# Output projection: the turned rows of the later token tiles go through two 512-column halves in the big accumulators

## The chip, the cores and the metric

The kernel runs on one core of a Trainium2 chip. The metric is the time of one execution on the device, in microseconds (us), as the median of several runs. The engines of a core are named as in the profile: PE is TensorE's matmul stream and PEld its weight loads, DVE is VectorE, ACT is ScalarE, POOL is GpSimd, and SP issues transfers. SBUF is the on-chip memory that the engines work from, PSUM the accumulators that PE writes, and DRAM the device's main memory.

## What is computed

One layer of a streaming encoder, for a prompt of 2048 tokens and for 8 x 16 sample tokens (one tile of 128), of 1024 columns each. Two token mixers (a chunked band attention and an mLSTM) give 512 columns each; the change lies in the product of the joined 1024 columns with `w_out` and the normalisation after it:

```python
h = rms_norm(x, norm_g[0])
z = h @ w_in
...
att = rms_norm(att, g_att)                      # 512 columns
...
mlstm_out = (hb * g_mlstm * sigmoid(ob))        # 512 columns
mix = jnp.concatenate([att, mlstm_out], axis=-1) @ w_out
x = x + rms_norm(mix, norm_g[1])
ffn, new_buf = conv_ffn(rms_norm(x, norm_g[2]), conv_buf, w_up, w_conv, b_conv, w_down)
x = x + rms_norm(ffn, norm_g[3])
```

All data is in 32-bit floats.

## The kernel before

The program runs through three stages, in about this order of time: the input projection with the attention and the mLSTM beside it (to about 1040 us), the output projection (`project`, about 1040 to 1306 us), and the feed-forward in three blocks of tokens.

A product of 32-bit numbers is made of three matmuls (`mm3`, lines 111 to 113): each operand is split into a high part, which ScalarE writes as a copy in a shorter format, and a low part, which VectorE writes as the difference. The three matmuls are high by high, high by low and low by high.

`project` goes through 17 tiles of 128 tokens, in the order 0 to 7, the sample tile (number 16, `SAMPLE`), 8 to 15. For one tile it does this:

- `load` brings the tile's 1024 columns into SBUF (`m`, in the trace `mr`). At tile 8 it first finishes the attention and mLSTM work and opens the pools of the feed-forward (`open_ffn`).
- `norm` takes the square sum of the 512 attention columns on ScalarE (L1021), the mean and its root on POOL (L94, L100), and scales those columns on VectorE (L1023).
- `turn_rows` turns the tile, since a matmul needs the contracted columns on the partitions: 8 transposes of 128 x 128 on PE (L83) into an accumulator, then the high part by a copy on ScalarE (L218) and the low part by a subtraction on VectorE (L219), both into `mt`.
- For each of two halves of the output columns, 8 x 3 matmuls sum into one 512-column accumulator (`wo` in the trace). Then VectorE multiplies it with the gain into `mx` (L1057), and ScalarE takes its square sum (L1059). The square's by-product is written to a place that is free at the time, `mx` for the first half and `mt` for the second.
- Root (L100), scaling and the residual (L1069), and the store (L1070).

The turn of the next tile is written down between the two halves of the current one. In the same loop `folds` (L1210 to L1217) prepares sums of `w_down` for the feed-forward: POOL issues loads and stores, VectorE adds (L1213). Until tile 8 the last attention and mLSTM work (`ms`, L716 to L733) runs beside the projection.

The accumulators come from one PSUM pool with two places for each kind: `ps_mm` gives 512 columns (tag `mm`) and `ps_big` 1024 (tag `big`). The projection's own accumulators are always `ps_mm`. `rows_to_T` takes the kind as `bank`: with `ps_big` itself it turns all 8 blocks into one accumulator and copies and subtracts 1024 columns at a time; with any other function it goes in two groups of four blocks, each with an accumulator, a copy and a subtraction of 512. Before the change tiles 0 to 7 use `ps_mm`, and the sample tile (number 16) and 8 to 15 use `ps_big`. The feed-forward uses `ps_big` for its accumulators `uec`, the attention for its scores and their transposes.

The order of the instructions on each engine is not that of the source: a planner lays it out when the program is built, from the source's order as priority and its own estimates of times, except where `keep_in_program_order` holds it. Each engine then works through its list in order. A tile in a place of a pool waits until the last reader of the place's former tile is done.

Of the kernel before, what the change touches and what calls it, by code (L numbers as in the profile page):

```python
# [50 lines left out]
def hymba_step(ctx: ExitStack, tc: tile.TileContext, I: dict, O: dict):  # L51
# [12 lines left out]
    def ps_big(name):  # L64
        return psum.tile([P, 1024], F32, tag="big", name=name)
# [16 lines left out]
    def transpose(out, in_, n=P):  # L82
        nc.tensor.transpose(out, in_, ident[:n, :n])  # L83
# [125 lines left out]
    def rows_to_T(hrow, chunk, j, name, bank):  # L209
        w = 4 if bank is not ps_big else KT  # L210
        for q in range(KT // w):
            pt = bank(f"{name}_pt{q}")
            for k in range(w):
                transpose(pt[:, k * P:(k + 1) * P], hrow[:, (w * q + k) * P:(w * q + k + 1) * P])
            ptv = pt.rearrange("p (k t) -> p k t", k=w)
            hv = chunk[:, 0, w * q:w * q + w, j * P:(j + 1) * P]
            lv = chunk[:, 1, w * q:w * q + w, j * P:(j + 1) * P]
            nc.scalar.copy(hv, ptv)  # L218
            nc.vector.tensor_tensor(lv, ptv, hv, op=ALU.subtract)  # L219
# [733 lines left out]

    wo = []
    g1 = []
    gatt = const.tile([P, 4], F32, name="gatt")

    def w_out_steps():
# [39 lines left out]
    def project(tiles):  # L998
# [25 lines left out]
            s.mt = mt[:, :2 * D].rearrange("p (a k n) -> p a k n", a=2, k=KT)  # L1024

        def turn_rows(s):
            rows_to_T(s.m, s.mt, 0, f"mT{s.t}", ps_mm if s.t < 8 else ps_big)

        fold, owed = folds(), [0.0]
        load(ss[0])  # L1030
        norm(ss[0])
        yield 0.0, 0.3
        turn_rows(ss[0])
        load(ss[1])
        yield 0.9, 1.2
        for n_, s in enumerate(ss):
# [7 lines left out]
            for hf in range(2):  # L1044
                c = slice(hf * 512, hf * 512 + 512)
                acc = ps_mm(f"wo{t}_{hf}")
                for k in range(KT):
                    mm3(acc, s.mt[:, 0, k, :], s.mt[:, 1, k, :], wo[k][0][:, c], wo[k][1][:, c],
                        start=(k == 0), stop=(k == KT - 1))
                    if k % 4 == 3:  # L1050
                        owed[0] += FOLD_RATE
                        while owed[0] >= 1:
                            owed[0] -= 1
                            next(fold, None)
                        yield 2.6, 0.5
                ssq = small.tile([P, 1], F32, tag="wssq", name=f"wssq{t}_{hf}")
                nc.vector.tensor_tensor(m[:, c], acc, g1[0][:, c], op=ALU.mult)  # L1057
                idle = m[:, 512:D] if hf == 0 else s.mt[:, 0, 0:4, :].rearrange("p k n -> p (k n)")
                nc.scalar.activation(idle, acc, AF.Square, accum_out=ssq)  # L1059
                if hf == 0:  # L1060
                    ssa = ssq
                    mean_square(ssa, ssq, D)
                    if nxt:
                        turn_rows(nxt)
                        if n_ + 2 < len(ss):
                            load(ss[n_ + 2])
                        yield 0.9, 1.2
# [957 lines left out]
```

## Time and profile before

| | us |
|---|---|
| median of 3 runs | 2727.55 |
| lowest and highest | 2724.9, 2730.89 |
| the profiled execution | 2730.95 |
| its span, first to last instruction | 2729.2 |

| engine | busy us | share of the span |
|---|---|---|
| PE | 2651.2 | 97% |
| DVE | 1862.9 | 68% |
| ACT | 1421.0 | 52% |
| POOL | 692.4 | 25% |

The times are those of one execution on the chip. A busy PE is a modelled figure, since matmuls overlap. In a row of the timeline the brackets hold how long the engine had been idle before the instruction and which instruction (engine, tile, line) released it. In a table by stretches, the columns are the length, the busy time of each engine, the granted clock of TensorE as a share of full speed, the share of the transfer engines, and GB/s. The granted clock over the whole span is 0.993.

### The profile page before, as it was taken

Reading aid. Unit: us, or ns where it says so; the run is one execution under the profiler, and the core shown is the slowest. Engines: PE = TensorE matmul, PEld = TensorE weight load, DVE = VectorE, ACT = ScalarE, POOL = GpSimd, SP = SyncE. Lnnn points to the kernel's source line nnn. Section 1 sums busy time; section 2 is a strip of 40 time slices with the busy share of each in tenths; the row PEclk is TensorE's granted clock in tenths of the full one; section 3 lists DMA queues with packets and bytes.
Section 4 is the critical chain, followed back from the end, with each engine's and each line's share of the span. In section 5 each row is a group of like instructions: output and inputs, shape, how many; then the busy total and the mean of one; then the engine's idle time right before and its main releaser. Section 6 shows DMA issues by size and latency. Waiting matters only on the chain. (4 is left out here: it accounts for less than half of the span.)

```text
span 2729.2 us, 47644 instructions
## 1 busy us (share of the span) xinstructions
PE 2651.2 (97%) x16459; PEld 2474.6 (91%) x16459; DVE 1862.9 (68%) x3519; ACT 1421.0 (52%) x2904; POOL 692.4 (25%) x1325
## 2 busy tenths in 40 slices
PE   7999999999999999999999999999999999999998
PEld 7899989998999998777999997899999878999976
DVE  5444555433556666566899997758888876999956
ACT  4345554433556665333555456655455665555554
POOL 1000001201000001354454551023333212556401
PEclk9999999999999999999999999999999999999999
DMA  5545465457644555598787668767886877798875
GB/s 174 156 124 149 125 183 158 151 155 252 194 139 134 152 151 158 178 294 287 281 241 236 204 206 294 237 187 202 228 220 175 256 237 239 213 253 232 259 250 180
DMA packets 333855, 555.73 MB, mean 204 GB/s; under 512 B 61906, under 2 KB 169518, under 8 KB 333294
## 3 DMA queue, kind: packets, MB, share of 16 engines
q1 hardware_dynamic: 250942, 405.06, 48.2%
q0 software_dynamic: 44080, 113.81, 14.5%
q10 hardware_dynamic: 38592, 33.83, 3.7%
q8 instruction: 129, 2.11, 0.3%
q14 instruction: 112, 0.92, 0.1%
HBM read 390.03 MB, written 172.22 MB: 206 GB/s over the span
## 5 line engine op out<-in xcount | busy, mean ns | idle before, releaser
L111 PE MATMUL uec<-B,wuh 128*128 128x384 f32 (+1 forms) x720 | 235.9, 328 | 5.3 <-DVE ug L1524 3.5
L112 PE MATMUL uec<-B,wuh 128*128 128x384 f32 (+1 forms) x720 | 235.1, 327 | 0.0
L113 PE MATMUL uec<-B,wul 128*128 128x384 f32 (+1 forms) x720 | 234.4, 327 | 0.0
L1353 ACT CAST wuh<-wu 128x512 fp32r<-128x512 f32 x255 | 141.7, 618 | 115.9 <-PE uec L112 113.5
L113 PE MATMUL dn<-wdh,al 128*128 128x512 f32 x462 | 186.8, 404 | 3.2 <-DVE al L1354 3.1
L111 PE MATMUL dn<-wdh,ah 128*128 128x512 f32 x462 | 184.3, 399 | 4.7 <-ACT ah L1353 3.3
L1354 DVE TENSOR_TENSOR al<-ar,ah 128x768 fp32r<-128x768 f32 (+2 forms) x141 | 108.5, 779 | 117.2 <-ACT ah L1353 113.9
L112 PE MATMUL dn<-wdl,ah 128*128 128x512 f32 x462 | 183.1, 396 | 0.0
L1353 ACT CAST ah<-ar 128x768 fp32r<-128x768 f32 (+2 forms) x141 | 96.2, 692 | 151.3 <-PE dnm L112 114.4
L1354 DVE TENSOR_TENSOR wul<-wu,wuh 128x512 fp32r<-128x512 f32 x255 | 164.4, 684 | 2.6 <-ACT wuh L1353 2.4
L111 PE MATMUL vo<-wi_h,hT 128*128 128x256 f32 x544 | 156.5, 288 | 1.9 <-ACT vo_st L244 1.8
L113 PE MATMUL vo<-wi_h,hT 128*128 128x256 f32 x544 | 155.2, 285 | 0.0
L112 PE MATMUL vo<-wi_l,hT 128*128 128x256 f32 x544 | 155.0, 285 | 0.0
L1354 DVE TENSOR_TENSOR wdl<-wdr,wdh 128x512 fp32r<-128x512 f32 x231 | 145.4, 685 | 7.6 <-ACT wdh L1353 7.4
L423 ACT ACTIVATE tmp<-tmp,mn 128x640 f32<-128x640 f32 (+4 forms) x128 | 97.7, 763 | 89.1 <-DVE mn L422 78.0
L111 PEld LDWEIGHTS uec<-B,wuh 128*128 128x128 f32 x720 | 135.1, 188 | 8.1 <-issue 3.5
L422 DVE CUSTOM_DVE_ANT_0 tmp<-s,nb 128x640 f32<-128x640 f32 (+4 forms) x128 | 94.1, 737 | 64.3 <-PE s L412 63.9
L112 PEld LDWEIGHTS uec<-B,wuh 128*128 128x128 f32 x720 | 135.2, 188 | 0.2
L113 PEld LDWEIGHTS uec<-B,wul 128*128 128x128 f32 x720 | 135.1, 188 | 0.0
L1353 ACT CAST wdh<-wdr 128x512 fp32r<-128x512 f32 x231 | 127.4, 620 | 13.2 <-PE uec L112 7.6
L435 DVE TENSOR_TENSOR ptl<-pt,pth 128x640 fp32r<-128x640 f32 (+4 forms) x128 | 93.8, 738 | 58.4 <-ACT pth L434 57.5
L111 PE MATMUL qk<-hT,wi_h 128*128 128x384 f32 (+1 forms) x384 | 128.2, 334 | 0.6 <-ACT gates L293 0.5
(473 smaller groups left out, 8968.6 us busy)
## 6 DMA issues: line engine op xcount, KB each, us to landing
wu<-in_w_up SPq DMA_DIRECT2D x220, 256.0 KB, 5.1
wu<-wsd SPq DMA_DIRECT2D x176, 256.0 KB, 4.9
wdr<-wtd SPq DMA_DIRECT2D x132, 256.0 KB, 5.8
wi_raw<-in_w_in SPq DMA_DIRECT2D x52, 512.0 KB, 4.2
wdr<-in_w_down SPq DMA_DIRECT2D x99, 256.0 KB, 4.6
wsd<-ws POOLq DMA_DIRECT2D x88, 256.0 KB, 4.9
ar<-ad_S SPq DMA_DIRECT2D x50, 384.0 KB, 3.9
kraw<-kTd SPq DMA_DIRECT2D x112, 128.0 KB, 3.3
```

The source lines that it names most:

```text
L111: nc.tensor.matmul(out, ah, bh, start=start, stop=False, skip_group_check=onto)
L112: nc.tensor.matmul(out, ah, bl, start=False, stop=False, skip_group_check=onto)
L113: nc.tensor.matmul(out, al, bh, start=False, stop=stop, skip_group_check=onto)
L422: nc.vector.tensor_tensor_reduce(o_, s_, b_, 1.0, 3e38, ALU.add, ALU.min, accum_out=mn)
L423: nc.scalar.activation(tmp[:, :n], tmp[:, :n], AF.Exp, bias=mn, scale=-1.0, accum_out=rsum[:, i % 4, hh:hh + 1])
L435: nc.vector.tensor_tensor(s.ptl[:, sl, qc], ptv, s.pth[:, sl, qc], op=ALU.subtract)
L1353: nc.scalar.copy(h, r)
L1354: nc.vector.tensor_tensor(l, r, h, op=ALU.subtract)
```

## The change

A constant `TURN_BIG = 4` takes the place of the 8 in `turn_rows`, and `ps_big` itself is no longer passed but a function that returns the first 512 columns of a big accumulator. As `rows_to_T` compares `bank` with `ps_big`, it now takes its other branch for every tile.

```diff
@@ -953,6 +953,7 @@
     wo = []
     g1 = []
+    TURN_BIG = 4
     gatt = const.tile([P, 4], F32, name="gatt")
...
@@ -1024,7 +1025,7 @@
         def turn_rows(s):
-            rows_to_T(s.m, s.mt, 0, f"mT{s.t}", ps_mm if s.t < 8 else ps_big)
+            rows_to_T(s.m, s.mt, 0, f"mT{s.t}", ps_mm if s.t < TURN_BIG else lambda name: ps_big(name)[:, 0:512])
```

So tiles 0 to 3 are as before. Tiles 4 to 7 still go in two groups of four blocks, but each group takes one of the two big accumulators and leaves the second half of it unused. The sample tile and tiles 8 to 15 go in two groups as well, each in a big accumulator of its own, with two copies and two subtractions of 512 columns in place of one each of 1024.

## The prediction

> **What bounds the kernel now.** I read the page's head first, then the busy time by stretches of the output projection, then the timeline of TensorE in that stretch for the idle time that ends at each turn, then ScalarE and VectorE around each of those gaps, and last the stretches behind the projection, to see whether time won there is kept.
>
> ```profile
> span 2729.2 us, 47644 instructions
> PE 2651.2 (97%) x16459; PEld 2474.6 (91%) x16459; DVE 1862.9 (68%) x3519; ACT 1421.0 (52%) x2904; POOL 692.4 (25%) x1325
> ...
> 1110.00:1310.00 200.00, 188.62 (x889) 151.21 (x889) 120.42 (x200) 72.95 (x176) 95.82 (x179) 0.97 0.83 273
> ...
> 1310.00:1330.00 20.00, 17.88 (x92) 17.30 (x92) 18.82 (x25) 11.20 (x15) 6.91 (x9) 0.91 0.81 312
> 1330.00:1550.00 220.00, 217.97 (x1244) 215.92 (x1243) 209.54 (x328) 111.59 (x177) 116.59 (x183) 1.00 0.74 228
> ```
>
> The columns of a stretch are its length, then busy us (and instructions) of PE, PEld, DVE, ACT and POOL, the granted clock, the DMA share and GB/s. TensorE is busy 97% of the span, so only its idle time and its slow time can be won. The change touches tiles 4 to 7, the sample tile and 8 to 15, which are turned between 1110 and 1310 us. There PE is idle 200.00 - 188.62 = 11.4 us, and the granted clock is 0.97. VectorE is at 60% and ScalarE at 36% there. Behind it, from 1330 on, PE is at 99% and VectorE at 95%.
>
> The wait of each turn, by the timeline (start, length, engine, line, and in brackets the idle time before it and what ended it):
>
> ```profile
> 1115.08 0.50 PE L111 MATMUL wo<-wo,mt 128*128 128x512 f32 x1 [0.27 <-DVE mt L219]
> ...
> 1128.54 0.49 PE L716 MATMUL ms<-mqk 128*128 128x128 f32 x2 [0.57 <-DVE num L733]
> ...
> 1144.81 0.66 PE L83 MATMUL mT_pt<-ident,mr 128*128 128x128 f32 x4 [0.65 <-ACT mx L1059]
> ...
> 1159.01 0.66 PE L83 MATMUL mT_pt<-ident,mr 128*128 128x128 f32 x4 [0.71 <-ACT mx L1059]
> 1160.47 0.50 PE L111 MATMUL wo<-wo,mt 128*128 128x512 f32 x1 [0.28 <-DVE mt L219]
> ...
> 1181.22 0.50 PE L111 MATMUL wo<-wo,mt 128*128 128x512 f32 x1 [1.16 <-ACT mt L218]
> 1185.14 0.79 PE L113 MATMUL wo<-wo,mt 128*128 128x512 f32 x1 [2.61 <-DVE mt L219]
> 1199.43 0.50 PE L111 MATMUL wo<-wo,mt 128*128 128x512 f32 x1 [0.46 <-ACT mt L218]
> 1254.04 0.50 PE L111 MATMUL wo<-wo,mt 128*128 128x512 f32 x1 [1.60 <-ACT mt L218]
> 1295.51 0.50 PE L113 MATMUL wo<-wo,mt 128*128 128x512 f32 x1 [0.90 <-DVE mt L219]
> ```
>
> Two kinds are to be seen. In tiles 4 to 7 the second four transposes wait for ScalarE's square of the projection (mx L1059), and the next accumulator waits for the subtraction (mt L219). Both are waits for a place among the two 512-column accumulators, which the turn shares with the projection. From the sample tile on, the matmuls of the next tile wait for the copy (L218) and the subtraction (L219) of its own turned rows.
>
> Where such idle time is long, the clock falls behind it:
>
> ```profile
> 1183.60:1190.40 6.80, 5.26 (x12) 4.13 (x13) 4.84 (x11) 0.00 (x0) 5.69 (x10) 0.51 0.98 387
> 1190.40:1196.40 6.00, 6.00 (x27) 4.82 (x26) 2.76 (x5) 0.69 (x2) 2.16 (x4) 0.99 0.91 269
> ...
> 1255.30:1258.70 3.40, 3.40 (x8) 2.72 (x9) 1.39 (x2) 1.00 (x2) 2.96 (x5) 0.51 1.03 414
> ...
> 1056.65 0.51 PE L111 MATMUL wo<-wo,mt 128*128 128x512 f32 x1 [1.15 <-ACT wo L983]
> ```
>
> Behind the sample tile's gaps the clock is 0.51 for 6.8 us: 12 matmuls take 5.26 us, where the next stretch does 27 in 6.00, so 12 would take 2.67. That is 2.6 us lost. Behind tile 12's gap of 1.60 us, 8 matmuls take 3.40, which at 27 in 6.00 would take 1.78: 1.6 us lost. A single gap of 1.15 (tile 0, at 1056.65) or 0.90 us (tile 15) has no such stretch behind it.
>
> On this the Trainium skill differs ("TensorE: Matmul & The Clock Gate", Part 1): it has the clock halved after at least one idle window of about 3.4 us, and warns of gaps above that. No gap of this stage is that long, so by that rule alone no clock time hangs on these turns and the sum below would be smaller by the two clock terms, -4.1 instead of -8.3; the trace shows the fall behind a gap of 1.60 us, and the trace decides.
>
> **The change part by part.** *Tiles 4 to 7.* The number of instructions stays; only the bank moves, from the 512-column accumulators to the two big ones. Nothing else uses the big ones here:
>
> ```profile
> L435 DVE TENSOR_TENSOR ptl<-pt,pth x128: 274/820/827, 101.6 to 1072.2; 128x640 fp32r<-128x640 f32 x96, 128x128 fp32r<-128x128 f32 x8, 128x256 fp32r<-128x256 f32 x8, 128x384 fp32r<-128x384 f32 x8
> ...
> L111 PE MATMUL uec<-B,wuh x720: 304/336/442, 1306.7 to 2579.8; 128*128 128x384 f32 x120, 128*128 128x320 f32 x60
> ```
>
> The attention read them last at 1072.2 us, and the feed-forward first writes them at 1306.7 (the third and fourth numbers are the first and last start). So the waits for a place go: 0.27 in tile 4, 0.65 in tile 6, 0.71 + 0.28 in tile 7. What is late next is the mLSTM's work on the same engine: in tile 5, where the transposes did not wait, PE stood 0.57 us for num (L733). In tile 7 the same num follows the transposes, so of its 0.99 I count 0.42. Together -1.3; the ends are 0 (num takes all the places) and -2.0 (all four rows).
>
> *The sample tile and 8 to 15.* Eight transposes into 1024 columns, one copy and one subtraction become two times four transposes, copies and subtractions of 512.
>
> ```profile
> L218 ACT CAST mt<-mT_pt x17: 578/1004/1017, 1113.7 to 1291.7; 128x1024 fp32r<-128x1024 f32 x9, 128x512 fp32r<-128x512 f32 x8
> L219 DVE TENSOR_TENSOR mt<-mT_pt,mt x17: 684/1214/1225, 1114.3 to 1294.2; 128x1024 fp32r<-128x1024 f32 x9, 128x512 fp32r<-128x512 f32 x8
> ```
>
> The columns are shortest, median and longest, in ns; the median is here one of the nine long ones, the shortest one of the eight short ones. Two copies of 512 take 2 x 0.58 = 1.16 us against 1.00, two subtractions 2 x 0.68 = 1.37 against 1.21: +0.16 a tile on each engine, +1.4 for nine, on engines that are idle 64% and 40% of the stage. I take 0 for them on the path; if that cover is gone they cost up to 1.4 each. In return the first half is ready sooner: the copy after 0.58 in place of 1.00, and it need wait for four transposes only, and the subtraction of half a row after 0.68 in place of 1.21. The first half feeds k = 0 to 3, 12 matmuls or 12 x 0.222 (27 in 6.00) = 2.7 us, which covers the second half's copy and subtraction.
>
> ```profile
> 1179.03 1.04 PE L83 MATMUL mT_pt<-ident,mr 128*128 128x128 f32 x8
> 1179.38 0.37 ACT L732 ACTIVATE num<-ms,colsp 128x129 f32<-128x129 f32 x1 [3.79 <-DVE cst L731]
> 1180.16 1.01 ACT L218 CAST mt<-mT_pt 128x1024 fp32r<-128x1024 f32 x1 [0.41 <-PE mT_pt L83]
> 1180.51 0.28 DVE L733 TENSOR_TENSOR num<-num,ms 128x129 f32<-128x129 f32 x1
> 1183.19 0.69 DVE L1213 TENSOR_TENSOR fold<-fold,fold 128x512 f32<-128x512 f32 x1 [2.40 <-issue]
> 1183.87 1.22 DVE L219 TENSOR_TENSOR mt<-mT_pt,mt 128x1024 fp32r<-128x1024 f32 x1
> ...
> 1252.99 1.00 ACT L218 CAST mt<-mT_pt 128x1024 fp32r<-128x1024 f32 x1
> 1254.03 1.23 DVE L219 TENSOR_TENSOR mt<-mT_pt,mt 128x1024 fp32r<-128x1024 f32 x1 [1.66 <-ACT mt L218]
> ...
> 1294.24 1.22 DVE L219 TENSOR_TENSOR mt<-mT_pt,mt 128x1024 fp32r<-128x1024 f32 x1
> ```
>
> Sample tile: ScalarE is free at 1179.75, so the first copy ends at 1180.33 in place of 1181.17. The subtraction stood behind a fold (L1213) that came to VectorE 2.40 us after the work before it. With the half ready at 1180.33, it can be queued behind num (ends 1180.79), before that fold, and end at 1181.5; the second half then comes behind the fold, at 1184.56, and holds PE some 0.3 us. The L113 of 1185.14 moves to about 1181.55, less 0.3: -3.3, and with so little idle time left the 2.6 of the slow clock goes too: -5.9. If the fold keeps its place, only 1.22 - 0.69 = -0.5 is left. I take -5.9: at 1252.99 and 1254.03 the subtraction follows its copy at once, as it would here.
>
> Tile 8: the 0.46 goes (-0.46), since the copy gains 0.41 and starts four transposes earlier. Tile 12: the gap of 1.60 shrinks by 1.00 - 0.58 to 1.18, the like of the 1.15 at 1056.65, so the slow clock goes: -0.4 - 1.6 = -2.0; the ends are -0.4 and -3.2 (the gap and its clock). Tile 15: the subtraction is late behind other VectorE work, and its half is 0.53 shorter: -0.5, to -0.9 if it is queued sooner.
>
> Against it stands the switch between transposes and matmuls:
>
> ```profile
> 1198.03 0.48 PE L111 MATMUL wo<-wo,mt 128*128 128x512 f32 x1
> 1198.35 0.39 PE L112 MATMUL wo<-wo,mt 128*128 128x512 f32 x1
> ```
>
> The first matmul behind a turn takes 0.32 to the next where 0.22 is usual: 0.1 more, for nine turns that become two groups each, +0.9. Last, the program's order is made by a planner from its own estimates, and moving these instructions lays the fold, the loads and the weights of the feed-forward anew. I count one new wait of the size of the rows 1.15 and 0.90: +1.0 (0 to 1.6 + 1.6, tile 12's gap with its clock).
>
> Sum: -1.3 - 5.9 - 0.5 - 2.0 - 0.5 + 0.9 + 1.0 = -8.3. The profiled execution took 2730.95 us (its span 2729.2 and 1.75 around it), which is 3.4 above the median of the runs, 2727.55. The sum gives 2722.7 for an execution like that one, and 2719.3 for the median, which I forecast.
>
> **The rivals.** *The fold keeps its place (R1).* VectorE is in order, and the row at 1183.19 shows that the planner expected the fold early. Then the sample tile gives -0.5 in place of -5.9: -8.3 + 5.4 = -2.9, 2724.7. Against it speaks only that the half is ready before num is done.
>
> *The clock term stays (R2).* If the re-laid gaps still sum to what makes the clock fall, only the idle time is won: -8.3 + 2.6 + 1.6 = -4.1, 2723.5. For it speaks that tile 12 keeps 1.18 us; against it the row at 1056.65. The rule of the Trainium skill named above comes to the same time by another way, and has no chance of its own beside the two slow stretches that the trace shows.
>
> *Nothing is kept behind the projection (R3).* The feed-forward starts on loads that follow the last projection matmul, and the DMA share is 0.83 in the stage.
>
> ```profile
> 1318.58 0.44 PE L112 MATMUL ua<-B,wuh 128*128 128x384 f32 x1 [1.96 <-DVE B L1199]
> ```
>
> Its wait is for the splitting of B on VectorE, which follows the projection's end, so it moves with it; were it bound by transfers or by VectorE's 95% instead, the gain would be lost: 2727.5.
>
> *Slower (R4).* A subtraction that is split has twice as many places where it can be queued behind a fold whose load is late. If the sample tile's stall stays and two more turns between 1206 and 1290 get one like it, at 2.61 + 2.6 = 5.2 each, the sum is -2.9 + 10.4 = +7.5: 2735.1. It decides from the second such turn on. For it: VectorE does folds all through the stage. Against: of the six turns there, only tile 12's made PE wait, and for the copy.
>
> **How the numbers follow.** Forecast 0.45, R1 0.22, R2 0.08, R3 0.10, R4 0.15. About 0.2% (5.5 us) is what a measurement of this kernel tells from no change. Faster by more is the forecast but for 0.02, and a third of R1 and R2, which lie 1.4 to 2.6 us from that bound: 0.43 + 0.10 = 0.53. Within it are the rest of R1 and R2, R3 and those 0.02: 0.32. R4 is slower: 0.15. The low end takes the far ends, -2.0 - 6.4 - 0.5 - 3.2 - 0.9 = -13.0 with no switch cost and no new wait, 2714.5, and 2.5 more for other waits that the new order may close; the high end leaves R4 out and holds R3 with a new gap and its clock, 2727.5 + 3.2 = 2731. The forecast's own range, without the other cases, is 2712 to 2722.
>
> **What would show it.** L218 and L219 34 times each with 512 columns, and none of 1024; no wait of a transpose for mx L1059 from tile 4 on; the wait for L218 at the sample tile under 0.5 us; a granted clock near 1.00 from 1175 to 1310 us where it was below; the projection's end some 8 us earlier and the end of the kernel by as much. It is wrong if the sample tile's L219 again stands behind a fold, if the slow stretch behind it is still there, or if new gaps over 1.5 us appear at tiles 9 to 14 or in the feed-forward.

## The result and the profile after

The changed kernel takes 2723.21 us (median of 11 runs, 2716.28 to 2727.21) where the kernel before, run beside it, takes 2730.89 (11 runs, 2724.9 to 2735.08): a ratio of 0.9967, with a 95% interval of 0.9956 to 0.9977. It is faster by 7.7 us by the medians and by 9.0 by the ratio (0.0033 x 2730.89). Two later comparisons of the same pair gave 0.9976 [0.9965, 0.9986] and 0.9971 [0.9960, 0.9981], which is 6.5 and 7.9 us. The forecast of 2719.3 us was set against a kernel before of 2727.55; beside this result the kernel before took 3.3 us more than that, so the gains, not the times, are to be compared. The line numbers of the changed kernel are one higher than before from line 956 on (L1059 is now L1060, L1140 L1141), while all the experiments below keep those of before.

The head of the profile after, and the same stretches as before:

```profile
span 2720.0 us, 47650 instructions
PE 2642.3 (97%) x16459; PEld 2470.0 (91%) x16459; DVE 1862.9 (68%) x3528; ACT 1422.9 (52%) x2913; POOL 699.5 (26%) x1325
...
1110.00:1310.00 200.00, 187.35 (x897) 151.88 (x894) 126.26 (x213) 81.50 (x191) 100.15 (x183) 0.97 0.84 288
1310.00:1330.00 20.00, 19.58 (x111) 19.33 (x112) 20.00 (x31) 8.08 (x14) 7.83 (x9) 1.00 0.60 208
```

The span is 9.2 us shorter, but the stretch from 1110 to 1310 looks no better than before: PE is idle 12.65 us there and the clock is again 0.97. It holds two opposite things. The first:

```profile
1105.00:1176.00 71.00, 71.00 (x354) 58.53 (x353) 39.67 (x83) 26.21 (x76) 28.84 (x60) 1.00 0.65 215
```

Through tiles 4 to 7 and into the sample tile PE does not stand at all, and the clock is full. The second is a new stall, shown by TensorE's timeline at tiles 9 and 10 and by the stretches around the fall of the clock there:

```profile
1194.43 0.50 PE L111 MATMUL wo<-wo,mt 128*128 128x512 f32 x1 [1.10 <-ACT mt L218]
1207.53 0.63 PE L1141 MATMUL h2T_pt<-ident,x2r 128*128 128x128 f32 x4 [1.38 <-DVE x2r L1133]
1210.09 1.09 PE L1141 MATMUL h2T_pt<-ident,x2r 128*128 128x128 f32 x8 [1.93 <-DVE x2r L1133]
1212.50 1.97 PE L83 MATMUL mT_pt<-ident,mr 128*128 128x128 f32 x8 [1.32 <-DVE mr L1024]
1215.42 1.12 PE L1141 MATMUL h2T_pt<-ident,x2r 128*128 128x128 f32 x4 [0.96 <-DVE t L1167]
1260.30 0.66 PE L1141 MATMUL h2T_pt<-ident,x2r 128*128 128x128 f32 x4 [1.78 <-DVE x2r L1133]
...
1207.60:1211.00 3.40, 1.47 (x12) 1.18 (x12) 2.13 (x3) 3.03 (x7) 3.08 (x7) 1.00 0.58 210
1211.00:1221.30 10.30, 7.85 (x25) 5.78 (x24) 9.86 (x14) 5.62 (x14) 8.46 (x13) 0.50 0.80 241
```

`h2T` are the transposes of the first rows of the feed-forward (`x2r`), which the planner lays between the projection's matmuls. They now wait for rows that are not ready, and behind these waits the clock is halved for 10.2 us. The first row of the fence is another wait: the matmuls of tile 9 stand for the copy of its turned rows.

To see what each part of the projection gained, I cut each trace at the same instructions: at the first turn, behind the last projection matmul of tiles 3, 7, 8, 10 and 15, and at the end of the program. The table gives the length of each stretch in us, and in brackets the time lost in it: PE's gaps, and half of PE's busy time under a halved clock (the 8.9 us behind PE's last matmul, the same in every trace within 0.1, are not counted). It is worked out from the starts and ends of the instructions and the rows of the clock in each trace. The column of the projection also holds tiles 0 to 3, which the change leaves as they are. The first three lines behind the two of before are three executions of the changed kernel; the others are the experiments.

```
                 tiles 4-7   sample, 8    9, 10        11-15       projection    feed-forward
before           58.2 (3.0)  33.8 (7.3)  26.7  (0.0)  67.0 (4.3)  264.1 (21.2)  1423.1 (21.0)
before_again     57.7 (2.6)  33.1 (6.6)  30.1  (3.3)  67.0 (3.6)  264.2 (20.4)  1421.9 (19.4)
after            53.0 (0.0)  26.4 (0.4)  38.7 (10.8)  64.9 (1.8)  258.9 (17.4)  1423.5 (21.2)
after_again      53.0 (0.0)  26.3 (0.2)  38.3 (10.3)  65.8 (2.5)  259.2 (17.3)  1420.1 (18.1)
after_third      53.4 (0.0)  26.3 (0.2)  37.3  (9.1)  64.7 (1.4)  257.2 (15.0)  1419.9 (17.4)
mid_halves       53.0 (0.0)  30.5 (4.4)  36.8  (9.1)  64.2 (1.3)  260.0 (18.7)  1419.1 (17.0)
mid_whole        55.0 (1.5)  33.7 (7.7)  33.2  (6.3)  64.0 (1.2)  261.5 (20.6)  1420.0 (18.3)
late_halves      57.9 (2.7)  28.6 (2.5)  28.1  (0.5)  62.6 (0.7)  254.3 (11.2)  1423.0 (18.9)
late_again       58.3 (3.1)  30.1 (4.1)  31.4  (3.8)  62.6 (0.7)  258.6 (15.8)  1425.8 (23.0)
sample_halves    57.9 (2.7)  31.3 (4.7)  26.9  (0.6)  67.1 (3.8)  259.6 (16.0)  1422.2 (18.7)
one_big          58.4 (3.2)  30.0 (4.6)  30.7  (2.5)  67.4 (3.6)  262.9 (18.3)  1424.9 (22.5)
lead14           53.0 (0.0)  26.3 (0.2)  28.6  (3.2)  73.9 (9.0)  256.1 (15.6)  1431.5 (26.6)
gap6             52.9 (0.0)  26.3 (0.2)  30.0  (4.6)  64.9 (0.3)  250.3 (9.8)   1439.0 (35.1)
actq             53.0 (0.0)  26.3 (0.2)  33.7  (8.0)  75.7(10.2)  263.7 (22.2)  1424.0 (21.7)
```

The projection is 5 to 7 us shorter in all three executions of the changed kernel. It wins some 5 us in tiles 4 to 7, 7 in the sample tile and tile 8 and 2 in tiles 11 to 15, and gives 7 to 12 back in tiles 9 and 10. The feed-forward is about as long as before. The profiled executions also differ by chance ahead of the change. PE's order is the same in both kernels until 3.5 tiles of the projection are done; the first matmul that differs starts at 1112.5 us in the first execution of before and at 1106.5 in the first of after. So 5.9 of the 9.2 us between these two spans lie ahead of the change, 4.4 of them ahead of the first turn. From the last common instruction to the end, the two executions of before take 1616.8 and 1618.1 us and the three of after 1613.5, 1610.6 and 1608.6: 3.3 to 9.5 us less, 6.5 between the means.

### The profile page after: what moved, and what is told of

The parts are those of the page before. It is cut to its first block, busy times and chain, and to the rows that moved or that the text cites. A ratio compares the mean times of both kernels' runs of the same rounds, so it can differ in the third digit from the quotient of the medians.

```text
span 2720.0 us, 47650 instructions
## 1 busy us (share of the span) xinstructions
PE 2642.3 (97%) x16459; PEld 2470.0 (91%) x16459; DVE 1862.9 (68%) x3528; ACT 1422.9 (52%) x2913; POOL 699.5 (26%) x1325
## 4 chain that ended last, share of the span: by engine, by line
PE 42%; DVE 3%; DMA 3%; issue 1%; ACT 1%; POOL 0%; DVEq 0%; POOLq 0%; ACTq 0%; SPq 0%
PE uec L111 5%; PE uec L112 5%; PE uec L113 5%; PE dn L113 3%; PE dn L111 3%; PE dn L112 3%; PE ua L113 3%; PE ua L111 3%; PE ua L112 3%; PE dnm L113 1%; PE dnm L112 1%; PE ub L113 1%; PE dnm L111 1%; PE ub L112 1%; PE ub L111 1%
## 5 line engine op out<-in xcount | busy, mean ns | idle before, releaser
L113 PE MATMUL uec<-B,wul 128*128 128x384 f32 (+1 forms) x720 | 234.4, 327 | 0.0
L113 PE MATMUL dn<-wdh,al 128*128 128x512 f32 x462 | 185.9, 402 | 3.9 <-DVE al L1355 3.9
L113 PE MATMUL vo<-wi_h,hT 128*128 128x256 f32 x544 | 155.2, 285 | 0.0
L113 PEld LDWEIGHTS uec<-B,wul 128*128 128x128 f32 x720 | 135.1, 188 | 0.0
L111 PE MATMUL qb<-hT,wi_h 128*128 128x384 f32 (+1 forms) x384 | 128.7, 335 | 0.0
```

What stands on the lines that cost most here:

```text
L111: nc.tensor.matmul(out, ah, bh, start=start, stop=False, skip_group_check=onto)
L113: nc.tensor.matmul(out, al, bh, start=False, stop=stop, skip_group_check=onto)
```

## Experiments: one part of the change at a time

Most edits are in line 1027, and there `half` stands for `lambda name: ps_big(name)[:, 0:512]`. The ratios are against the kernel before on the same chip, with 95% intervals.

**Tiles 4 to 7 alone (mid_halves).**

```diff
-rows_to_T(s.m, s.mt, 0, f"mT{s.t}", ps_mm if s.t < 8 else ps_big)
+rows_to_T(s.m, s.mt, 0, f"mT{s.t}", ps_mm if s.t < 4 else half if s.t < 8 else ps_big)
```

> Only tiles 4 to 7 take the big accumulators in halves; the sample tile and 8 to 15 are turned as before, 1024 columns at once. Theory A (each part of the change takes away its own waits): PE's waits of tiles 4 to 7 (3.6 us between 1110 and 1175 in the kernel before) are gone, the sample tile's wait for its copy and subtraction is still there, and the feed-forward's first transposes, which the planner lays in one bunch at the start of tile 11's place here as in the changed kernel, make PE wait about 5 us: 3 to 6 us less than before. Theory B (all of the gain is tiles 4 to 7): 9 us less, as in the changed kernel. Theory C (only the re-laid order matters): anything, and no relation to the wait rows of tiles 4 to 7.

Measured: 2721.57 against 2726.34 us, 0.9981 [0.9968, 0.9994], 5.2 us, as theory A has it. The waits of tiles 4 to 7 are gone (0.0). At tiles 9 and 10 as much is lost as in the changed kernel (9.1), so a loss of that size comes with this part of the change and does not need the halves of the later tiles. It is not the same wait: no `h2T` waits here, and PE stands for the copies and subtractions of the turns of tiles 9 and 10 (1.13, 2.29 and 2.88 us) and 1.08 us ahead of tile 10's transposes. The late fold, too, is still seen; it now stands ahead of the subtraction of tile 8. VectorE and then TensorE in this kernel:

```profile
1183.17 0.69 DVE L1213 TENSOR_TENSOR fold<-fold,fold 128x512 f32<-128x512 f32 x1 [2.24 <-issue]
1184.04 1.22 DVE L219 TENSOR_TENSOR mt<-mT_pt,mt 128x1024 fp32r<-128x1024 f32 x1
...
1183.35 0.50 PE L111 MATMUL wo<-wo,mt 128*128 128x512 f32 x1 [2.38 <-ACT mt L218]
1185.31 0.80 PE L113 MATMUL wo<-wo,mt 128*128 128x512 f32 x1 [0.49 <-DVE mt L219]
```

**The sample tile and 8 to 15 alone (late_halves, and again as late_again).**

```diff
-rows_to_T(s.m, s.mt, 0, f"mT{s.t}", ps_mm if s.t < 8 else ps_big)
+rows_to_T(s.m, s.mt, 0, f"mT{s.t}", ps_mm if s.t < 8 else half)
```

> Only the sample tile and 8 to 15 go in two halves through the big accumulators; tiles 4 to 7 stay in the 512-column accumulators. Theory A: the waits of tiles 4 to 7 stay (about 3 us), the waits behind the sample tile's and tile 12's turn shrink below 1 us each and the half clock behind them goes: 5 to 8 us less than before. Theory B: no change within 3 us.

> Only the sample tile and 8 to 15 in halves, once more, beside the changed kernel on the same chip. By the first profile its projection is 4.7 us shorter than the changed kernel's, since the bunch of the feed-forward's first transposes does not come about. If that holds: as fast as the changed kernel or up to 4 us faster, 5 to 9 us less than before. If the first profile was chance: slower than the changed kernel by the 3 us of waits in tiles 4 to 7.

Measured: 2720.80 against 2726.34 us, 0.9984 [0.9970, 0.9999], and 2719.09 against 2727.12, 0.9989 [0.9969, 1.0009]. Tiles 4 to 7 lose their 2.7 to 3.1 us as before; the sample tile and tile 8 gain 3 to 5; tiles 11 to 15 gain 4.4; and tiles 9 and 10 lose 0.5 and 3.8, no more than in the two executions of before. By the ratios the whole change is worth 6.5 to 9.0 us and its two parts 5.2 and 3.0 to 4.4: the intervals can't tell their sum from the whole. The gain of this part is clear of no change in the first comparison only, just, and below the 5 us that both expectations had at least. The short projection of the first profile, 254.3 us, did not come back (258.6): that was chance.

**The sample tile alone (sample_halves).**

```diff
-rows_to_T(s.m, s.mt, 0, f"mT{s.t}", ps_mm if s.t < 8 else ps_big)
+rows_to_T(s.m, s.mt, 0, f"mT{s.t}", ps_mm if s.t < 8 else half if s.t == SAMPLE else ps_big)
```

> Only the sample tile goes in two halves. If its subtraction is no longer held behind a fold (the prediction's term of 5.9 us): 4 to 6 us less than before, with the granted clock at 1.00 behind that tile. If the fold keeps its place: 0.5 us less, which cannot be told from no change, and the clock there falls as before.

Measured: 2724.33 against 2726.34 us, 0.9989 [0.9975, 1.0003], 3.0 us by the ratio, below the 4 to 6 expected and too small to be told from no change. But its VectorE rows answer a point of the prediction:

```profile
1173.12 0.28 DVE L733 TENSOR_TENSOR num<-num,ms 128x129 f32<-128x129 f32 x1
1173.32 0.68 DVE L219 TENSOR_TENSOR mt<-mT_pt,mt 128x512 fp32r<-128x512 f32 x1
1175.67 0.69 DVE L1213 TENSOR_TENSOR fold<-fold,fold 128x512 f32<-128x512 f32 x1 [1.67 <-issue]
1176.28 0.68 DVE L219 TENSOR_TENSOR mt<-mT_pt,mt 128x512 fp32r<-128x512 f32 x1
```

The first half is subtracted right behind num and ahead of the late fold, the second half behind it, as was forecast, and the stall of 2.61 us at the sample tile is gone. Tile 8 then waits instead:

```profile
1187.07 0.50 PE L111 MATMUL wo<-wo,mt 128*128 128x512 f32 x1 [1.16 <-ACT mt L218]
1188.82 0.50 PE L111 MATMUL wo<-wo,mt 128*128 128x512 f32 x1 [1.01 <-ACT mt L1059]
```

so that the stretch keeps 4.7 us of lost time, 1.6 of it under a halved clock.

**Which half of the idea counts: the accumulator or the split (mid_whole, one_big).** In mid_whole tiles 4 to 7 go whole into one big accumulator. In one_big the sample tile and 8 to 15 are copied and subtracted in two halves, but both halves lie in one big accumulator.

```diff
 mid_whole:
-rows_to_T(s.m, s.mt, 0, f"mT{s.t}", ps_mm if s.t < 8 else ps_big)
+rows_to_T(s.m, s.mt, 0, f"mT{s.t}", ps_mm if s.t < 4 else ps_big)
 one_big:
-        w = 4 if bank is not ps_big else KT
+        w = 4 if bank is not ps_big or name[0] == "m" else KT
...
-            pt = bank(f"{name}_pt{q}")
+            if bank is ps_big and w == 4:
+                whole = bank(f"{name}_pt") if q == 0 else whole
+                pt = whole[:, q * 512:q * 512 + 512]
+            else:
+                pt = bank(f"{name}_pt{q}")
```

> Tiles 4 to 7 go whole, 1024 columns, through one big accumulator; the rest as before. It tells the bank from the split for these tiles. If the waits for a place among the 512-column accumulators are what tiles 4 to 7 lose: the waits for the square of the projection are gone as with halves and it gains 2 to 5 us, less up to 1 us a tile where the longer copy and subtraction make the next tile wait. If the shorter halves matter as much: no gain, or a loss of 1 to 3 us.

> The sample tile and 8 to 15 go in two halves of 512 columns, but both halves in one big accumulator as before; tiles 4 to 7 as before. It tells the split of the copies from the second accumulator. If the split alone makes the chain shorter: as with the two accumulators, 3 to 6 us less than before. If the accumulators are what matters (a copy of the first half has to wait until all eight transposes have left the accumulator): no change within 2 us.

Measured: mid_whole 2722.58 against 2724.36 us, 0.9988 [0.9975, 1.0002]; one_big 2728.79 against 2724.36, 1.0016 [1.0002, 1.0029]. Neither the ratio of mid_whole nor its difference from mid_halves is clear of noise. In its trace the waits of tiles 4 to 7 for a place, and the one for num, are all gone, and two new ones come, 0.82 us for the copy and 0.67 for the subtraction of 1024 columns: the place is won by the larger accumulator, and the halves take away the wait for the longer copy and subtraction.

For the later tiles, the split in one accumulator did not make the kernel faster. The expectation had the reason wrong: the first copy does start right behind its four transposes, but the second four stand in PE's list behind the first half's subtraction. VectorE and PE's weight loads in one_big:

```profile
1175.29 0.68 DVE L223 TENSOR_TENSOR mt<-mT_pt,mt 128x512 fp32r<-128x512 f32 x1
1176.03 0.43 PEld L83 LDWEIGHTS mT_pt<-ident,mr 128*128 128x128 f32 x4 [0.20 <-DVE mt L223]
```

(L223 is the subtraction there.) So it is in all nine turns: the second transposes come 0.1 to 0.8 us behind the end of the first subtraction, where in the changed kernel they come 1.5 to 5.2 us ahead of it. The second copy therefore starts 2.4 to 4.6 us behind the first, in place of 0.5 to 1.1. At the sample tile and tile 8 that does no harm (30.0 us against 28.6 and 30.1 in late_halves and late_again); in tiles 11 to 15 the gain is missing (67.4 against 62.6). Why the kernel is slower by 4 us rather than equal is not settled: its lost time, 18.3 + 22.5 us, is about that of before, but the projection without it is 0.8 to 1.7 us longer.

**Both kernels once more (after_again, after_third, before_again).** The change is written without the constant, in one line, so that the lines keep their numbers; the kernel before is as it was.

> The changed kernel once more, with its lines numbered as before's, to be timed beside the others and profiled a second time. Theory A: 7 to 11 us less than before, about the sum of the two parts (5.2 for tiles 4 to 7 alone, 4.4 for the sample tile and 8 to 15 alone); in the profile no wait of PE in tiles 4 to 7, under 1 us at the sample tile and tile 8, and again 5 us or more of waits where the feed-forward's first transposes stand. Rival: the first profile's start, 4.4 us ahead of before where the order of the instructions is the same, was a chance of that execution, and the gain is only some 2 to 5 us.

> The changed kernel on the chip of the three other runs of this group, as their measure: 6 to 9 us less than before, with the stretch from the first turn to the end of tile 15 at 259 us within 1 as in its first two profiles.

> The kernel before, unchanged, for a second profile: how far the stretches of the projection vary from one execution to the next with the same order of instructions. If the waits are a matter of the order, the stretch from the end of tile 3 to the end of tile 15 is 185.6 us within 2, with the wait behind the sample tile's turn above 2 us and the clock falling behind it; if they are chance, that stretch differs by 5 us or more.

Measured: 2718.09 against 2724.36 us, and 2717.55 against 2727.12, with the ratios given above; the kernel before in one more execution 2722.88. The lines of the table show what holds: the gains at tiles 4 to 8 and the stall at tiles 9 and 10 come back each time, and the time lost under a halved clock does not. Three bounds were missed by little: 6.5 us where after_again had 7 to 11, 257.2 us for the projection where after_third had 259 within 1, and 187.9 us from tile 4 on where before_again had 185.6 within 2. In the kernel before that clock time was 6.1 us of the projection in the one execution and 3.3 in the other.

## Experiments: the new stall

Its parts can be read in the traces. In the kernel before, no transpose of these rows waited in the first execution (one for 0.49 us in the other), and the loads of the first two (SP, L1112) were issued when 8.6 of the 17 tiles had their matmuls done. In the changed kernel 10.0 tiles were done:

```profile
1193.42 1.28 SPq L1112 DMA_DIRECT2D x2r<-x2d  x2
...
1211.10 0.60 PE L1140 MATMUL h2T_pt<-ident,x2r 128*128 128x128 f32 x4
1212.70 0.60 PE L1140 MATMUL h2T_pt<-ident,x2r 128*128 128x128 f32 x4
```

```profile
1192.96 1.23 SPq L1113 DMA_DIRECT2D x2r<-x2d  x2
...
1205.80 1.06 ACT L1129 ACTIVATE B<-x2r 128x1024 fp32r<-128x1024 f32 x1 [0.65 <-DMA x2r<-x2d]
1206.10 1.28 DVE L1133 SCALAR_TENSOR_TENSOR x2r<-x2r,n_rs,g 128x1024 f32<-128x1024 f32 x1 [4.83 <-POOL n_rs L100]
1208.51 1.06 ACT L1129 ACTIVATE B<-x2r 128x1024 fp32r<-128x1024 f32 x1 [0.37 <-DMA x2r<-x2d]
1208.75 1.28 DVE L1133 SCALAR_TENSOR_TENSOR x2r<-x2r,n_rs,g 128x1024 f32<-128x1024 f32 x1 [1.36 <-POOL n_rs L100]
```

(The first fence is of before, the second of after.) Counted from the first turn, the loads are issued 151.4 and 149.2 us later in the two executions of before, and 155.3 to 156.2 us later in the three of after. The place of these loads in SP's list has moved back by one tile. Wherever they go out on SP, the last store of the mLSTM (L685) and a load of the residual (L1043) stand ahead of them; the residual is that of tile 8 in before and that of tile 9 in after, which goes out when the store of the sample tile has landed (154.3 to 155.3 us, where tile 7's store had landed at 148.2 and 150.3). The loads stand one tile back in all five such kernels in which tiles 4 to 7 use the big accumulators (after, mid_halves, mid_whole, lead14, gap6), and in none of the others. In the same five, the planner has the last 13 to 15 mLSTM matmuls behind tile 7; that these draw the loads along fits the order, but no run moved them alone. PE's list has changed too: the first four groups of `h2T` stood at 9.9, 10.0, 10.3 and 10.5 tiles in before, and all four at 11.0 in after. In before the first row was scaled 5.2 us ahead of its transposes (1205.9 and 1211.1 us); in after PE is there first, and waits for the scaling of the rows and for the work on the blocks that it turned before.

That is not all of the stall. Of the 6.5 to 8.6 us of gaps in tiles 9 and 10, the `h2T` groups wait for 2.6 to 4.3 us, tile 9's matmuls for 1.1 to 3.0 and the turn of tile 10 for 0.7 to 2.7. Tile 9's wait has to do with a late fold (VectorE and ScalarE, after):

```profile
1191.83 0.69 DVE L1214 TENSOR_TENSOR fold<-fold,fold 128x512 f32<-128x512 f32 x1 [3.66 <-DMA fold<-in_w_down]
1192.44 0.69 DVE L1058 TENSOR_TENSOR mx<-wo,norm_row 128x512 f32<-128x512 f32 x1
1193.21 0.60 ACT L1060 ACTIVATE mx<-wo 128x512 f32<-128x512 f32 x1 [9.25 <-issue]
1193.80 1.07 ACT L218 CAST mt<-mT_pt 128x512 fp32r<-128x512 f32 x2
```

VectorE stands 3.66 us for the fold's load, with the product (L1058) behind it; ScalarE's square (L1060) starts when the product is done and has the copies of tile 9 behind it, whose transposes ended at 1192.6. The same rows stand in all three executions of after; VectorE stands 3.1 to 3.7 us there. Three kernels tried to win the stall back. All three hold the whole change.

**The feed-forward's first rows, loads and turns, 8 steps later in the source (lead14).**

```diff
-        pipes[:] = [Pipe(h2_units(0, lead=6)), Pipe(iter([]))]
+        pipes[:] = [Pipe(h2_units(0, lead=14)), Pipe(iter([]))]
```

> The changed kernel with the feed-forward's first turns begun 8 steps later (lead 14 in place of 6), so that the planner spreads their first transposes over tile 11's place and not in one bunch. If that bunch costs what it seems to in the changed kernel's profile (5.6 us of waits between 1207 and 1216 and 10.2 us at half clock, together about 10 us): 2711 to 2716, 7 to 12 us less than the changed kernel. If the waits only move (the rows' loads and squares are late anyway, or VectorE holds the feed-forward's start): within 3 us of the changed kernel.

Measured: 2726.78 against 2726.34 us, 0.9994 [0.9980, 1.0007]: the change's gain is gone, which neither side of the expectation had. No `h2T` of the projection waits any more, and tiles 9 and 10 lose only 3.2, 2.6 of it at tile 9's turn; but tiles 11 to 15 lose 9.0 and the feed-forward 26.6. ScalarE, in order, has a square in its list whose row has not landed, and the copy behind it is late:

```profile
1268.99 1.06 ACT L1128 ACTIVATE B<-x2r 128x1024 fp32r<-128x1024 f32 x1 [8.91 <-DMA x2r<-x2d]
1270.05 1.05 ACT L218 CAST mt<-mT_pt 128x512 fp32r<-128x512 f32 x2
...
1270.67 0.79 PE L111 MATMUL wo<-wo,mt 128*128 128x512 f32 x1 [5.77 <-ACT mt L218]
```

**More room between the loads and the transposes (gap6).**

```diff
-            if not late:
+            for _ in range(6 if late else 1):
                 yield 0.0, 0.0
```

> The changed kernel with six empty steps between the loads of the feed-forward's first rows and their first transposes (the loads stay where they are, the transposes stand later in the source), so that the planner lays the first unit's transposes over tiles 10 and 11's places in four parts. Theory: PE waits at tile 10 in the changed kernel (6.9 and 8.6 us in its two profiles) because the transposes stand where the planner expects the rows, while the loads land later. Then the idle time of tiles 9 and 10 falls below 3 us and the projection ends 3 to 6 us earlier than in the changed kernel; the end of the program by as much, unless the feed-forward waits for the later rows. Rival (the work of these units is bound by VectorE and ScalarE wherever it stands): the waits move to tiles 11 to 15 and the feed-forward, and the time is that of the changed kernel within 2 us, or worse as with the lead of 14.

Measured: 2725.09 against 2727.12 us, 0.9986 [0.9973, 0.9999], where the changed kernel in the same comparison took 2717.55. For the projection the theory held, and by more than expected: no `h2T` waits there, the one gap left in tiles 9 and 10 is the 2.9 us of tile 9's turn, and the projection is the shortest of all, 250.3 us, 7 to 9 less than with the change alone. The feed-forward takes it back: 1439.0, with 35.1 lost against 17.4 to 21.2. The stretches behind the projection, of this kernel and then of the changed one, and two of this kernel's waits:

```profile
1290.00:1330.00 40.00, 34.28 (x176) 31.80 (x176) 35.81 (x51) 23.90 (x35) 13.99 (x23) 0.96 0.77 287
1330.00:1400.00 70.00, 66.29 (x362) 65.15 (x361) 61.67 (x98) 31.80 (x51) 33.94 (x55) 0.95 0.74 232
...
1372.40 0.48 PE L111 MATMUL uec<-B,wuh 128*128 128x384 f32 x1 [2.08 <-DVE ug L1524]
1468.26 0.66 PE L111 MATMUL uec<-B,wuh 128*128 128x384 f32 x1 [2.98 <-DVE ug L1524]
```

```profile
1300.00:1330.00 30.00, 27.88 (x158) 27.30 (x159) 30.00 (x43) 17.61 (x26) 14.20 (x17) 1.00 0.74 278
1330.00:1400.00 70.00, 69.78 (x400) 69.25 (x399) 67.11 (x105) 35.96 (x57) 37.53 (x59) 1.00 0.78 243
```

VectorE, busy 67.11 of 70.00 us there in the changed kernel, prepares what the feed-forward's matmuls need. PE arrives earlier and meets work that is not ready. That the work put off at tiles 9 to 12 is what VectorE lacks here is my reading; no run took it away alone.

**The loads on ScalarE's queue (actq).** They had stood behind other transfers on SP.

```diff
-        nc.sync.dma_start(ffn.g2, I["norm_g"][2:3, :].broadcast_to([P, D]))
+        nc.scalar.dma_start(ffn.g2, I["norm_g"][2:3, :].broadcast_to([P, D]))
...
-                    fetch = nc.sync.dma_start(rows_[t], x2d[t])
+                    fetch = (nc.scalar if late else nc.sync).dma_start(rows_[t], x2d[t])
```

> The changed kernel with the loads of the feed-forward's first rows and of its gain issued from ScalarE's queue in place of SP's, where they stand behind a load that waits for a store to land. If SP's queue is what makes these rows late: they are issued at once when their place is free, 3 to 5 us earlier, and the idle time of tiles 9 and 10 falls by about as much; 2 to 5 us less than the changed kernel. If the place comes free late (the mLSTM's last store) or the landing of 8 us is what counts: under 1.5 us.

Measured: 2725.70 against 2727.12 us, 0.9993 [0.9982, 1.0003]. The first two loads are issued 155.1 us behind the first turn, where the changed kernel had 155.3 to 156.2. That does not clear SP's list, since ScalarE's has a wait of its own ahead of them:

```profile
1194.42 0.60 ACT L1059 ACTIVATE mx<-wo 128x512 f32<-128x512 f32 x1 [9.95 <-issue]
1194.84 0.94 ACTq L1112 DMA_DIRECT2D x2r<-x2d  x1
```

ScalarE stands 9.95 us for the square of tile 8's first half, and the loads go out right behind it; the residual's load, which stood ahead of them on SP, went out at 152.5. How early the rows could be fetched stays open. The next two loads come 20 us later than these (SP: 2 us), and another stall stands at tile 11:

```profile
1232.26 1.09 PE L1140 MATMUL h2T_pt<-ident,x2r 128*128 128x128 f32 x4 [2.41 <-DVE x2r L1132]
```

So the stall at tiles 9 and 10 is real, but none of the three turned it into time: the expectation that some of its 9 to 11 us can simply be won fell. None of them took out tile 9's late fold. No kernel here is shown to beat the changed one.

## Where the prediction was right and where wrong

**The time and the sign.** Forecast: 8.3 us faster; measured: 9.0, 6.5 and 7.9 by the three ratios. The sum agrees, and in part by luck, since its terms do not. The lost time from tile 4 on, which is what the sum priced, fell from 14.6 and 16.1 us to 10.7 to 13.0, by some 3 us and not by 8.3: the gains came to some 11.5, where 10.2 were forecast, and the new waits took 6 to 11 of it back, where 1.0 was forecast. The rest of the 6.5 us between the traces is in no term: some 0.6 in waits late in tile 3, 1.5 as PE runs the same matmuls of the projection in less time, for which no cause is shown, and 1.3 in the feed-forward, which is no more than its executions differ. Two figures of the prediction are also not what its text works out: the four rows of tiles 4 to 7 add up to 1.9 and not 2.0, and the low end has 6.4 for the sample tile, for which nothing is worked out beyond 5.9.

**Instructions.** As promised, the groups by tile show halves alone:

```profile
L218 ACT CAST mt<-mT_pt x34: 569/587/603, 1038.8 to 1283.3; 128x512 fp32r<-128x512 f32 x34
L219 DVE TENSOR_TENSOR mt<-mT_pt,mt x34: 679/684/695, 1040.5 to 1285.7; 128x512 fp32r<-128x512 f32 x34
```

**Tiles 4 to 7, forecast -1.3, ends 0 and -2.0.** Too small. All 2.6 to 3.0 us of waiting went, those for num as well: I had kept most of num's wait as the thing that is late next, and taken only the four rows over a quarter of a microsecond. A wait for the scaling of tile 6's row (0.62 us, mr L1023, at 1142.8) was overlooked; it stands in five of the six executions that turn tiles 4 to 7 as before. The stretch is shorter by some 2.2 us more, as 15 mLSTM matmuls moved behind it; that is no gain.

**Sample tile and tile 8, forecast -5.9 - 0.46.** Right in size: 7.3 and 6.6 us of lost time became 0.2 to 0.4. The step behind it is shown by sample_halves, where the first half passes the late fold. But in the whole change it is not this step alone. The turn of the sample tile lies earlier, and tile 8's subtractions, too, stand ahead of the fold that was late (rows of VectorE, after):

```profile
1181.18 0.69 DVE L219 TENSOR_TENSOR mt<-mT_pt,mt 128x512 fp32r<-128x512 f32 x1
1182.04 0.68 DVE L219 TENSOR_TENSOR mt<-mT_pt,mt 128x512 fp32r<-128x512 f32 x1
1182.64 0.68 DVE L1214 TENSOR_TENSOR fold<-fold,fold 128x512 f32<-128x512 f32 x1
```

Each part of the change alone leaves 2.5 to 4.7 us there; only both together leave next to nothing.

**Tiles 12 and 15, forecast -2.5.** Lost time in tiles 11 to 15 went from 4.3 and 3.6 to 1.4 to 2.5. The size is right; of what is left, 1.78 us (at 1260.30) is no wait of a turn but of `h2T`.

**The switches, forecast +0.9.** Not seen: without the lost time the projection takes 242.9 and 243.8 us before and 241.5 to 242.2 after, with the same 1233 matmuls and transposes. The step that failed is the count: the nine turns did not become two groups each. In PE's list eight of them still go in one run of 8 transposes, and the sample tile's in 5 and 3. In one_big all nine do go in two groups, and there the projection without the lost time takes 244.6 us, 0.8 to 1.7 more than before, with four matmuls of the feed-forward in it: a price of that size is possible where the groups do part.

**One new wait, forecast +1.0 (0 to 3.2).** This step failed. I priced the planner's new order by the two largest single rows that had no fall of the clock behind them. What came is a train of waits, 6.5 to 8.6 us of gaps in tiles 9 and 10, and 1.7 to 3.9 under a halved clock, against 0 and 3.3 in all before: 6 to 11 us more, beyond the far end of its range. The `h2T` groups are about half of the gaps; tile 9's turn behind a late fold and tile 10's turn are the rest. My text named it as what would make the prediction wrong ("new gaps over 1.5 us at tiles 9 to 14"). The rows that could have warned of it are those ahead of the loads on SP: the loads stand behind the mLSTM's last store and behind a residual's load that waits for a store of the projection, so PE can run ahead and they cannot.

**The rivals.** R1, the fold keeps its place: the four rows of sample_halves exclude it. R2, the clock term stays: in part. It was 6.1 in the execution I worked from but 3.3 in the other one of before, and 1.7 to 3.9 after. So 2.8 us of clock time differ between two executions of the same kernel, and the 4.2 that I priced as a cost of these turns was partly chance. R3, nothing is kept: the feed-forward's lengths, 1419.9 to 1423.5 against 1421.9 and 1423.1, exclude it for this change; but in gap6 it holds, where 8 us won in the projection were all given back. R4, subtractions behind late folds: one such turn is in mid_halves. In the whole change its mechanism came at one turn, tile 9's, and by a way that the rival did not have: the late fold holds a product, that the square, and that the copy. It took 1.1, 2.0 and 3.0 us of gaps, and in after_again a fall of the clock; the rival needed two such turns at 5.2 each. For the subtraction itself the matmuls of L113 wait 0.2 us in all in after and in after_third, and 3.0 in after_again, 1.6 of it at tile 15.

## What to carry to other kernels

A faster stage does not start the next one earlier when the next stage's first loads stand in a queue behind something that is not faster; look for what stands ahead of those loads, and price the new order by that chain, not by the size of gaps that are there today. Where two stages share one kind of accumulator and another kind lies idle, moving the turn to the idle kind takes the waits away; give each half an accumulator of its own, since halves in one made the second half's transposes wait for the first half's subtraction, and the kernel was no faster. And judge a part by stretches cut at the same instructions in several executions: two spans of one execution each differed here by 5.9 us ahead of the change and by 3.3 behind it.

## What the runs showed of the hardware

**When the clock falls.** The prediction took it that a gap of 1.60 us brings a fall and one of 1.15 doesn't. Tile 2's gap shows that the length doesn't decide. Before, and then after:

```profile
1083.29 0.66 PE L83 MATMUL mT_pt<-ident,mr 128*128 128x128 f32 x4 [1.80 <-ACT mx L1059]
...
1081.30:1084.70 3.40, 1.60 (x10) 1.16 (x9) 2.37 (x6) 1.40 (x4) 0.20 (x1) 1.00 0.63 201
1084.70:1088.10 3.40, 3.40 (x10) 2.62 (x9) 0.79 (x2) 0.55 (x3) 0.00 (x0) 0.50 0.70 211
```

```profile
1079.01 0.66 PE L83 MATMUL mT_pt<-ident,mr 128*128 128x128 f32 x4 [1.72 <-ACT mx L1060]
...
1078.00:1081.40 3.40, 2.39 (x12) 1.97 (x13) 2.57 (x6) 1.70 (x5) 0.20 (x1) 1.00 0.71 213
1081.40:1084.80 3.40, 3.40 (x17) 2.71 (x16) 0.00 (x0) 0.25 (x2) 0.00 (x0) 1.00 0.40 139
```

In all fourteen executions the falls behind 60 us start on a grid with a step of 3.413 us, within 0.002 us, so closely that the time can be cut into windows by it. Of the windows at full clock in which PE was busy under 40%, 39 of 39 were followed by a fall; of those with 40 to 50%, 27 of 50; with 50 to 55%, 5 of 30; with more, 1 of 10660 (at 61%). The grid was fitted to the falls of each execution, so this is a reading of the traces, not a test. The stretches above are cut at it: in before the gap lies within one window, in after 0.7 us of it lie in the window that ends at 1078.0 and 1.0 in the next. By it a gap of 1.7 or 1.8 us can halve the clock if it lies within one window and does nothing if it is shared by two, which is why the same order of instructions fell in one execution and not in the next. The Trainium skill ("TensorE: Matmul & The Clock Gate", Part 1) has the fall after at least one idle window of about 3.4 us. The step of the grid agrees; a window does not have to be idle, as the row with 1.60 us busy of 3.40 shows, and about half of it idle was often enough.

**Executions of the same program.** The first turn came at 1032.1 to 1042.0 us in the fourteen executions, whose instructions up to there are in the same order on PE: 9.9 us of chance, more than the whole change.
